# Feed-forward output of a four-layer decoder: seven block products per chunk in place of eight

## The chip, the cores and the metric

The kernel runs on one core of a Trainium2 chip. The metric is the device time of one execution in microseconds (us), of which several runs are taken. One execution was also recorded by the hardware profiler. The engines are TensorE (PE; PEld is its weight load), VectorE (DVE), ScalarE (ACT), GpSimd (POOL) and SyncE (SP), which issues the transfers (DMA).

## What is computed

Four decoder layers on 256 tokens of width 1024, in float32. Each layer has a feed-forward part, a token mixer (attention, gated linear attention, RWKV-7, attention) and another feed-forward part. The change is in the feed-forward parts alone, eight in all:

```python
def swiglu(x, w_in, w_out):
    gate, up = jnp.split(x @ w_in, 2, axis=-1)
    return (jax.nn.silu(gate) * up) @ w_out
...
        ff = swiglu(rmsnorm(h, g[0]), ffn_w_in[layer, 0], ffn_w_out[layer, 0])
        h = h + 0.5 * rmsnorm(ff, g[1])
```

`w_in` is 1024 x 5632, `w_out` is 2816 x 1024.

## The kernel before, in words

Each matmul of two float32 operands is made of three: an operand is split into a rounded part `hi` (a ScalarE copy) and a rest `lo` (a VectorE subtract), and `mm3` (L599) adds hi x hi, hi x lo and lo x hi. `weight` (L581) loads a 128 x 512 tile of weights and splits it so.

A feed-forward stage (`ffn`, L739) goes through the 2816 hidden values in 11 chunks of 256. The first two chunks (`OLD`) are done by `tokens` (L760) for each half of 128 tokens by itself, so that the first half can begin while the stage before still works on the second. There gate and up come out as 128 tokens x 512, go through VectorE, and are transposed on TensorE. The other nine chunks take both halves together: gate and up come out with the hidden values on the partitions, two PSUM banks per chunk, 96 matmuls of 256 columns. After the activation, `out` multiplies the hidden values with the chunk's 256 x 1024 piece of `w_out`. As blocks of 128 that is a 2 x 2 times 2 x 2 product: token half t, half i of the output columns, half j of the hidden values, 8 block products of three matmuls of 512 columns each. They add up in four PSUM banks, `acc[t][i]`, over all chunks; the other four banks rotate. At the end `postnorm` (L705) normalises each half's sum and adds it to the residual `h`.

No instruction stands where the program text has it. Every call is recorded with a due time, and a planner (`schedule`, L325) orders the calls of each engine by prices (`price`, L272) and by the free slots of each kind of tile: 87 `m` tiles of 512 columns, 14 `hf` of 256, 8 PSUM banks `ps`. Splits and loads may be put up to 24 us ahead of their due time. Where the planner sees TensorE idle behind a bank's release, it fills the time with matmuls of a tile of ones, which nothing reads (`o.fill`, L421, in fillers of 214 ns by its own price). All calls come out of `emit` (L458), so in the profile they share one line, L466, and the fillers have L464. An engine works its instructions off in the planned order: one that is late holds up what stands behind it.

## Time and profile before

| | us |
|---|---|
| median of 3 runs | 2063.19 (2063.02 to 2063.63) |
| the profiled execution | 2061.41 |
| its span, first to last instruction | 2059.4 |
| TensorE busy | 2041.0 (99%) |
| VectorE busy | 1415.6 (69%) |
| ScalarE busy | 1127.9 (55%) |
| GpSimd busy | 120.2 (6%) |
| DMA queue of SyncE | 352.78 MB, 55.1% of 16 engines' span |

A group of instructions is named by line, engine, operation and tiles (out<-in). Busy time is the union of the group's instructions; two that follow each other overlap, so that twelve of 0.69 us can take less than 12 x 0.69. A float32 matmul that is not split shows as two instructions, a filler too.

### The profile page before, as it was taken

The page shows a single profiled execution, that of the slowest core. Times are in us where ns is not written, and L with a number is a line of the kernel's source. Part 1 is how long each engine was busy: PE and PEld are TensorE (multiplying, and loading weights), DVE is VectorE, ACT ScalarE, POOL GpSimd, SP SyncE. Part 2 cuts the span into 40 slices and gives each one's busy share as a digit, 9 for nine tenths or more (in the row PEclk, how much of TensorE's full clock was granted, in tenths as well). Part 3 has the DMA queues.
Part 4 walks back from the last instruction along what each step waited for, and adds up shares of the span by engine and source line. Part 5 has one row for each costly group of instructions (what it writes and reads, how often), then busy time and mean ns, then how long its engine had stood idle before and what let it go on. Part 6 is the DMA issues. An engine that isn't in the chain of part 4 may idle for free.

```text
span 2059.4 us, 38914 instructions
## 1 busy us (share of the span) xinstructions
PE 2041.0 (99%) x14250; PEld 1792.2 (87%) x14250; DVE 1415.6 (69%) x2684; ACT 1127.9 (55%) x2408; POOL 120.2 (6%) x185
## 2 busy tenths in 40 slices
PE   9999999999999999999999999999999999999998
PEld 7998779998998888998899878888998899877997
DVE  7666886657666897666756797687666755688663
ACT  7444675446544965545554576566444544566442
POOL 0000000002000000000100022130000000000000
PEclk9999999999999999999999999999999999999999
DMA  9556365666555365566655521456566566536551
GB/s 299 179 184 200 125 191 173 189 186 196 176 184 186 117 186 184 175 188 201 190 179 179 155 87 63 126 168 189 180 185 209 168 186 204 163 122 204 174 185 66
DMA packets 288207, 355.25 MB, mean 173 GB/s; under 512 B 24156, under 2 KB 207632, under 8 KB 288016
## 3 DMA queue, kind: packets, MB, share of 16 engines
q1 hardware_dynamic: 288016, 352.78, 55.1%
q8 instruction: 111, 1.82, 0.4%
q14 instruction: 80, 0.66, 0.1%
HBM read 351.64 MB, written 1.05 MB: 171 GB/s over the span
## 4 chain that ended last, share of the span: by engine, by line
PE 86%; DVE 6%; ACT 2%; issue 2%; POOL 2%; DMA 1%; SPq 0%; DVEq 0%; POOLq 0%; ACTq 0%
PE ps L466 85%; DVE m L466 4%; POOL ti L466 2%; ACT m L466 1%; ACT junk L466 1%; DVE h L466 1%; DVE ti L466 1%; DMA h<-in_x_dram 0%; POOL m L466 0%; DMA m<-in_rwkv_a_dram 0%; PE ps L464 0%; DVE hf L466 0%; DMA m<-in_swa_w_o_dram 0%; SPq L466 0%; DMA m<-in_swa_w_qkv_dram 0%
## 5 line engine op out<-in xcount | busy, mean ns | idle before, releaser
L466 PE MATMUL ps<-m,m 128*128 128x256 f32 (+5 forms) x12128 | 1846.1, 316 | 3.9 <-ACT m L466 2.3
L466 PEld LDWEIGHTS ps<-m,m 128*128 128x128 f32 (+2 forms) x12128 | 1596.9, 185 | 192.6 <-issue 11.8
L466 ACT ACTIVATE m<-m 128x512 fp32r<-128x512 f32 (+3 forms) x1542 | 848.9, 617 | 608.7 <-DVE m L466 530.9
L466 DVE TENSOR_TENSOR m<-m,m 128x512 fp32r<-128x512 f32 (+2 forms) x1414 | 895.5, 687 | 101.6 <-ACT m L466 98.2
L466 DVE TENSOR_TENSOR m<-ps,m 128x512 f32<-128x512 f32 (+1 forms) x220 | 151.1, 690 | 377.4 <-PE ps L466 324.3
L466 ACT ACTIVATE m<-ps 128x512 f32<-128x512 f32 (+4 forms) x179 | 93.1, 547 | 133.4 <-PE ps L466 131.6
L466 POOL TENSOR_TENSOR ti<-ti,nhalf 128x1 f32<-128x1 f32 (+2 forms) x60 | 55.4, 924 | 1683.9 <-DVE ti L466 1516.1
L466 PE MATMUL ps<-m,hf 128*128 128x512 f32 (+1 forms) x716 | 124.5, 323 | 0.0
L466 PEld LDWEIGHTS ps<-m,hf 128*128 128x128 f32 (+1 forms) x716 | 83.1, 165 | 18.0 <-issue 3.1
L466 DVE SCALAR_TENSOR_TENSOR m<-m,m 128x512 f32<-128x512 f32 x102 | 69.7, 691 | 21.2 <-ACT m L466 14.9
L466 PE MATMUL ps<-ident,m 128*128 128x128 f32 (+1 forms) x344 | 57.5, 278 | 1.5 <-DVE m L466 0.6
L466 ACT ACTIVATE m<-ps,gT 128x128 fp32r<-128x128 f32 (+1 forms) x192 | 53.3, 378 | 3.6 <-PE ps L466 3.1
L466 ACT ACTIVATE hf<-ps,ti 128x256 f32<-128x256 f32 x32 | 15.1, 473 | 70.3 <-PE ps L466 70.2
L466 PEld LDWEIGHTS ps<-ident,m 128*128 128x128 f32 (+1 forms) x344 | 40.5, 142 | 14.9 <-DVE m L466 3.7
L466 POOL TENSOR_SCALAR_AFFINE_SELECT m<-m 128x512 f32<-128x512 f32 (+1 forms) x54 | 39.0, 742 | 190.4 <-ACT m L466 190.2
L466 DVE SCALAR_TENSOR_TENSOR m<-ps,gT,m 128x128 fp32r<-128x128 f32 x176 | 48.6, 343 | 1.9 <-ACT m L466 1.5
L466 ACT ACTIVATE junk<-h 128x512 bf16<-128x512 f32 x48 | 30.3, 631 | 22.1 <-DVE h L466 19.5
L466 ACT ACTIVATE junk<-ps 128x512 bf16<-128x512 f32 (+1 forms) x48 | 27.2, 567 | 27.3 <-PE ps L466 26.6
L466 DVE SCALAR_TENSOR_TENSOR h<-m,ti,h 128x512 f32<-128x512 f32 x48 | 34.2, 748 | 11.1 <-POOL ti L466 11.1
L466 DVE TENSOR_TENSOR m<-m,ps 128x256 f32<-128x256 f32 (+1 forms) x56 | 23.5, 455 | 26.1 <-PE ps L466 25.6
L466 ACT ACTIVATE hf<-ps 128x256 fp32r<-128x256 f32 (+4 forms) x54 | 19.8, 370 | 32.9 <-PE ps L466 32.9
L466 DVE SCALAR_TENSOR_TENSOR hf<-hf,ps 128x256 f32<-128x256 f32 x32 | 13.4, 418 | 33.9 <-ACT hf L466 33.8
(95 smaller groups left out, 574.3 us busy)
## 6 DMA issues: line engine op xcount, KB each, us to landing
m<-in_ffn_w_in_dram SPq DMA_DIRECT2D x704, 256.0 KB, 4.1
m<-in_ffn_w_out_dram SPq DMA_DIRECT2D x352, 256.0 KB, 5.1
m<-in_swa_w_qkv_dram SPq DMA_DIRECT2D x48, 256.0 KB, 3.6
m<-in_rwkv_w_rkv_dram SPq DMA_DIRECT2D x48, 256.0 KB, 3.2
m<-in_gla_w_in_dram SPq DMA_DIRECT2D x40, 256.0 KB, 3.5
m<-in_swa_w_o_dram SPq DMA_DIRECT2D x32, 256.0 KB, 2.8
m<-in_norm_g_dram SPq DMA_DIRECT2D x24, 256.0 KB, 5.2
m<-in_gla_w_o_dram SPq DMA_DIRECT2D x16, 256.0 KB, 2.7
```

Source lines behind the costliest of these rows:

```text
L466: getattr(getattr(self.nc, o.eng), fn)(*[fix(v) for v in args], **{k: fix(v) for k, v in kw.items()})
```

## The change

The four blocks of the hidden values and the four of `w_out` are combined so that seven block products per chunk are enough. `weights` makes four sums T of weight blocks on GpSimd (128 x 512 each) and splits three plain blocks and the four sums: seven splits per chunk where four were. `hidden` makes four sums S of hidden blocks on GpSimd (128 x 128 each) and splits three plain blocks and the four sums. `products` adds the seven products up in seven PSUM banks over all chunks. Gate and up of 128 hidden values share the eighth bank: it is filled, read and filled again in each chunk, and VectorE's and ScalarE's work on gate and up is done in two halves. The products follow one chunk behind. In the last four chunks (`TAIL`) the products 7 and 4, which only the second token half needs, are put off to the end. There seven VectorE sums and a copy make the four output blocks from the seven banks. The weights for a half chunk of gate and up are loaded in two transfers of 128 KB each (`load_half`), in place of one of 256 KB.

```diff
-MID = 8000.0
+MID = 16000.0
...
-LAST = 0
+LATE = 6000.0
+TAIL = 4
+
+AHEAD = 8000.0
+RESERVE = 16
...
         if fn == "tensor_tensor":
-            return 300 + 165.0 * n, 0.0
+            return 300 + 165.0 * n if args[3] == ALU.pow else 120 + 1.1 * n, 0.0
...
-                            if j >= len(f) or (t.first > front and occ[t.kind][front:t.first].max() + j >= bufs[t.kind]):
+                            keep = RESERVE if t.kind == "m2" and o.window is not None and o.key > now + AHEAD else 0
+                            if j + keep >= len(f) or (t.first > front and occ[t.kind][front:t.first].max() + j >= bufs[t.kind]):
...
-        nc.sync.dma_start(view(x) if view else x, src)
+        y = view(x) if view else x
+        for o, i in zip(y, src) if isinstance(src, list) else ((y, src),):
+            nc.sync.dma_start(o, i)
...
+        def load_half(c, j, k):
+
+            cols = slice(c * CH + j * P, c * CH + (j + 1) * P)
+            return self.weight([w_in[:, k + i, :, cols] for i in range(2)],
+                               lambda x: [x[:, i * CH:(i + 1) * CH].rearrange("p (s n) -> p s n", s=2) for i in range(2)])
...
+        def split(x, dt):
+
+            hi, lo = dt(), dt()
+            nc.scalar.activation(hi[:], x, AF.Copy)
+            nc.vector.tensor_tensor(lo[:], x, hi[:], ALU.subtract)
+            return hi, lo
+
+        def weights(c):
+
+            b = {}
+            nc.kind = "load"
+            for j in range(2):
+                for i in range(2):
+                    w = b[2 - j, i + 1] = self.m2()
+                    nc.sync.dma_start(w[:], w_out[:, 2 * c + j, i * 512:(i + 1) * 512])
+            nc.kind = "split"
+            T = {n: self.m2() for n in (1, 2, 3, 4)}
+            for n, x, y in ((1, b[1, 2], b[1, 1]), (2, b[2, 2], T[1]), (4, b[2, 1], T[2]), (3, b[2, 2], b[1, 2])):
+                GT(T[n][:], x[:], y[:], ALU.subtract)
+            r = {n: split(w[:], lambda: self.m2(dt=F32R)) for n, w in (
+                (1, b[1, 1]), (2, b[2, 1]), (3, b[2, 2]), (5, T[1]), (6, T[2]), (7, T[3]), (4, T[4]))}
+            nc.kind = None
+            return r
...
+        def hidden(th):
+
+            a12, a22, a11, a21 = (th[:, j, t, :] for j in range(2) for t in range(NT))
+            S = self.m2([P, 4, P])
+            s = [None] + [S[:, n, :] for n in range(4)]
+            GT(s[1], a21, a22, ALU.add)
+            GT(s[2], s[1], a11, ALU.subtract)
+            GT(s[3], a11, a21, ALU.subtract)
+            GT(s[4], a12, s[2], ALU.subtract)
+            three = th[:].rearrange("p j t n -> p (j t) n")[:, :3]
+            x = split(three, lambda: self.m2([P, 3, P], F32R))
+            y = split(S[:], lambda: self.m2([P, 4, P], F32R))
+            return {n: tuple(v[:, m, :] for v in z) for n, z, m in (
+                (1, x, 2), (2, x, 0), (4, x, 1), (5, y, 0), (6, y, 1), (7, y, 2), (3, y, 3))}
+
+        acc = {n: self.psum() for n in range(1, 8)}
+
+        def products(c, which):
+            w, x = wt[c], hid[c]
+            for n in which:
+                self.mm3(acc[n][:], x[n], tuple(v[:] for v in w[n]), c == 0, c == NCH - 1)
...
-            gh, gl = self.hf([P, CH], F32R), self.hf([P, CH], F32R)
-            nc.scalar.activation(gh[:], q[:, :CH], AF.Copy)
-            nc.vector.tensor_tensor(gl[:], q[:, :CH], gh[:], ALU.subtract)
-            for i in range(2):
-                for j in range(2):
-                    out(t, c, j, i, gh[:, j * P:(j + 1) * P], gl[:, j * P:(j + 1) * P])
-
-        rs, eps, acc, row = [None] * NT, [None] * NT, [None] * NT, self.m2()
+            nc.scalar.activation(ths[c][:, :, t, :], q[:, :CH].rearrange("p (j n) -> p j n", j=2), AF.Copy)
...
+        FIRST, SECOND = (1, 6, 5, 2), (3, 7, 4)
+        for c in range(OLD):
+            wt[c], hid[c] = weights(c), hidden(ths[c])
+            if c < OLD - 1:
+                products(c, FIRST + SECOND)
+        todo = list(range(OLD - 1, NCH))
+        for c in range(OLD, NCH):
+            for j in range(2):
+                p, half = self.psum(), {}
+                for s in range(2):
                     for k in range(KD):
...
+                        if k % 2 == 0 and s == 0:
+                            half[k // 2] = load_half(c, j, k)
+                        w, n = half[k // 2], (k % 2 * 2 + s) * P
+                        self.mm3(p[:, s * N:(s + 1) * N], (w.hi[:, n:n + P], w.lo[:, n:n + P]),
...
-            sg, th = self.m2([P, 2, N]), self.m2([P, 2, N])
-            two = lambda x: x[:].rearrange("p (j n) -> p j n", j=2)
-            nc.vector.tensor_tensor(sg[:], two(gate), row[:, :N].unsqueeze(1).to_broadcast([P, 2, N]), ALU.mult)
...
-            gh, gl = self.m2([P, 2, N], F32R), self.m2([P, 2, N], F32R)
-            nc.scalar.activation(gh[:], th[:], AF.Copy)
-            nc.vector.tensor_tensor(gl[:], th[:], gh[:], ALU.subtract)
...
+                sg, th, up = self.hf([P, N]), self.hf([P, N]), self.hf([P, N])
+                nc.vector.tensor_tensor(sg[:], p[:, :N], row[:, :N], ALU.mult)
+                nc.scalar.activation(up[:], p[:, N:], AF.Copy)
+                nc.scalar.activation(th[:], sg[:], AF.Tanh)
+                nc.vector.scalar_tensor_tensor(th[:], th[:], 1.0, sg[:], ALU.add, ALU.mult)
+                nc.vector.tensor_tensor(ths[c][:, j].rearrange("p t n -> p (t n)"), up[:], th[:], ALU.mult)
+                if j == 1:
+                    wt[c] = weights(c)
+                    hid[c] = hidden(ths[c])
+                products(todo[0], (FIRST, SECOND if todo[0] < NCH - TAIL else SECOND[:1])[j])
+            todo.pop(0)
         g = self.gain(n0 + 1, 16.0)
...
+        for n in FIRST + SECOND[:1]:
+            for c in todo:
+                products(c, (n,))
+        end = nc.base + nc.pe
+        s1, u2, u4 = self.m2(), self.m2(), self.m2()
+        c1, c2 = self.pair(), self.pair()
+        TT = nc.vector.tensor_tensor
+        nc.scalar.activation(s1[:], acc[1][:], AF.Copy)
+        TT(u2[:], s1[:], acc[6][:], ALU.add)
+        TT(u4[:], u2[:], acc[5][:], ALU.add)
+        TT(c1[0][:], s1[:], acc[2][:], ALU.add)
+        TT(c1[1][:], u4[:], acc[3][:], ALU.add)
+        self.postnorm(0, [x[:] for x in c1], g, eps[0][:, :1])
+        nc.base, nc.pe, nc.shift = end, 0.0, LATE
+        for n in SECOND[1:]:
+            for c in range(NCH - TAIL, NCH):
+                products(c, (n,))
+        TT(u2[:], u2[:], acc[7][:], ALU.add)
+        TT(c2[1][:], u4[:], acc[7][:], ALU.add)
+        TT(c2[0][:], u2[:], acc[4][:], ALU.add)
+        self.postnorm(1, [x[:] for x in c2], g, eps[1][:, :1])
         nc.shift = 0.0
```


How the planner's order moves, at three places. Names are the program's tiles with their numbers: `ps3` is the fourth PSUM bank, `m` an SBUF tile of 512 columns, `hf` one of 256.

First place, TensorE in the loop over chunks, where one half of gate and up is done and the bank is needed again. Before (`ps3_19` is gate, `ps6_21` up, `ps5_18` an output bank):

```order
L466 MATMUL ps3_19_642<-m226_27_205,m221_106_540 128x256
L466 MATMUL ps5_18_530<-m23_91_452,hf10_11_685 128x512
L466 MATMUL ps3_19_642<-m226_27_205,m211_103_507 128x256
L466 MATMUL ps3_19_642<-m230_31_223,m211_103_507 128x256
L466 MATMUL ps3_19_642<-m226_27_205,m222_107_544 128x256
L466 MATMUL ps6_21_737<-m219_20_180,m20_88_442 128x256
L466 MATMUL ps5_18_530<-m280_81_421,hf11_12_691 128x512
L466 MATMUL ps6_21_737<-m224_25_197,m20_88_442 128x256
L466 MATMUL ps6_21_737<-m219_20_180,m26_94_464 128x256
L466 MATMUL ps6_21_737<-m219_20_180,m21_90_449 128x256
L466 MATMUL ps6_21_737<-m224_25_197,m21_90_449 128x256
```

Now (`ps3_31` and `ps3_32` are two uses of the one bank; `ps5`, `ps1`, `ps4` are products 3, 7 and 4):

```order
L471 MATMUL ps3_31_1575<-m226_27_205,m232_311_1406 128x256
L471 MATMUL ps5_21_643<-m243_243_1071,m238_319_1456 128x512
L471 MATMUL ps5_21_643<-m211_275_1243,m238_319_1456 128x512
L471 MATMUL ps5_21_643<-m243_243_1071,m245_320_1464 128x512
L471 MATMUL ps1_22_657<-m268_252_1131,m238_319_1456 128x512
L471 MATMUL ps1_22_657<-m278_280_1263,m238_319_1456 128x512
L471 MATMUL ps1_22_657<-m268_252_1131,m245_320_1464 128x512
L471 MATMUL ps4_23_665<-m255_254_1140,m218_315_1434 128x512
L471 MATMUL ps4_23_665<-m263_281_1271,m218_315_1434 128x512
L471 MATMUL ps4_23_665<-m255_254_1140,m257_317_1445 128x512
L471 MATMUL ps3_32_1678<-m219_20_180,m274_308_1394 128x256
```

Two banks took turns, and single products stood between the matmuls of up; now nine products (twelve behind the other half) stand between two uses of one bank.

Second place, VectorE and GpSimd in the loop. VectorE before, from up of one chunk to gate of the next:

```order
L466 TENSOR_TENSOR m238_157_780<-ps6_21_737,m238_157_780 128x512
L466 TENSOR_TENSOR m275_170_837<-m234_163_807,m278_164_809 128x512
L466 TENSOR_TENSOR m256_172_848<-m238_157_780,m283_171_840 128x512
L466 TENSOR_TENSOR m271_175_857<-m272_166_816,m281_167_819 128x512
L466 TENSOR_TENSOR m255_178_866<-m267_168_823,m240_169_828 128x512
L466 TENSOR_TENSOR m253_181_875<-m268_173_853,m286_174_855 128x512
L466 TENSOR_TENSOR m23_182_879<-m282_176_861,m22_177_863 128x512
L466 TENSOR_TENSOR m280_183_884<-m277_179_869,m229_180_871 128x512
L466 TENSOR_TENSOR m20_186_910<-m25_184_906,m284_185_908 128x512
L466 TENSOR_TENSOR m29_189_922<-m26_187_918,m21_188_920 128x512
L466 TENSOR_TENSOR m27_192_934<-m24_190_930,m215_191_932 128x512
L466 TENSOR_TENSOR m210_193_939<-ps0_23_826,m213_102_504 128x512
```

VectorE now, from gate of one half chunk to gate of the next:

```order
L471 TENSOR_TENSOR hf0_29_1775<-ps3_32_1678,m25_93_457 128x256
L471 TENSOR_TENSOR m268_386_1779<-m247_348_1572,m20_360_1643 128x512
L471 SCALAR_TENSOR_TENSOR hf2_31_1784<-hf2_31_1784,hf0_29_1775 128x256
L471 TENSOR_TENSOR m218_387_1791<-hf1_30_1781,hf2_31_1784 128x256
L471 TENSOR_TENSOR m215_398_1815<-m250_353_1613,m280_362_1652 128x512
L471 TENSOR_TENSOR m239_401_1826<-m23_354_1617,m273_364_1673 128x512
L471 TENSOR_TENSOR m236_404_1847<-m270_355_1625,m216_365_1675 128x512
L471 TENSOR_TENSOR m248_409_1885<-m253_373_1715,m217_376_1724 128x512
L471 TENSOR_TENSOR m247_411_1890<-m251_374_1718,m234_377_1729 128x512
L471 TENSOR_TENSOR m235_413_1899<-m267_375_1721,m232_380_1743 128x512
L471 TENSOR_TENSOR m229_415_1904<-m286_378_1733,m243_382_1749 128x512
L471 TENSOR_TENSOR hf3_32_1907<-ps3_33_1824,m25_93_457 128x256
```

GpSimd now, one chunk; it had nothing there before:

```order
L471 TENSOR_TENSOR m215_340_1552<-m282_339_1550,m283_338_1548 128x512
L471 TENSOR_TENSOR m236_341_1554<-m233_337_1546,m282_339_1550 128x512
L471 TENSOR_TENSOR m239_342_1556<-m233_337_1546,m215_340_1552 128x512
L471 TENSOR_TENSOR m260_344_1560<-m242_336_1544,m239_342_1556 128x512
L471 TENSOR_TENSOR m252_368_1686<-m28_335_1542 128x128 x2
L471 TENSOR_TENSOR m252_368_1686<-m252_368_1686,m28_335_1542 128x128
L471 TENSOR_TENSOR m252_368_1686<-m28_335_1542,m252_368_1686 128x128
```

The read of a bank comes twice per chunk, with eight to nine splits queued between two of them; GpSimd has four sums of 512 columns in a row (T) and then four of 128 (S).

Third place, TensorE at the end of a stage. Before (`h0` is the residual of the first token half, whose transposes open the next stage):

```order
L466 MATMUL ps7_17_522<-m256_428_2144,m222_484_2446 128x512
L466 MATMUL ps5_18_530<-m270_431_2156,m258_483_2442 128x512
L466 MATMUL ps5_18_530<-m20_432_2158,m258_483_2442 128x512
L466 MATMUL ps5_18_530<-m270_431_2156,m222_484_2446 128x512
L466 MATMUL ps5_18_530<-m218_435_2171,m258_483_2442 128x512
L466 MATMUL ps5_18_530<-m247_436_2174,m258_483_2442 128x512
L466 MATMUL ps0_39_2514<-ident_77,h0_74 128x128 x4
L466 MATMUL ps4_40_2522<-ident_77,h0_74 128x128 x4
L466 MATMUL ps5_18_530<-m218_435_2171,m222_484_2446 128x512
L466 MATMUL ps3_41_2537<-m240_446_2248,m253_499_2528 128x512
```

Now (L469 is the fillers' line of the changed kernel):

```order
L471 MATMUL ps4_23_665<-m217_581_2735,m211_616_2887 128x512
L471 MATMUL ps4_23_665<-m23_595_2804,m211_616_2887 128x512
L471 MATMUL ps4_23_665<-m217_581_2735,m274_618_2896 128x512
L469 MATMUL ps3_42_2975<-ones_76 128x128 x13
L471 MATMUL ps3_42_2975<-ident_77,h0_74 128x128 x4
L471 MATMUL ps7_43_2996<-ident_77,h0_74 128x128 x4
L469 MATMUL ps0_44_3009<-ones_76 128x128
L471 MATMUL ps0_44_3009<-m255_583_2746,m269_640_3003 128x512
```

Products of the second token half stood before and behind the first half's transposes; now thirteen fillers stand there. In the whole program the fillers go from 48 to 115, beside 9 of the same kind at the start of both.

## Rows read from the trace of the kernel before

**Rows 1.** The page, parts 1 and 2: busy time, TensorE's granted clock in tenths.

```profile
PE 2041.0 (99%) x14250; PEld 1792.2 (87%) x14250; DVE 1415.6 (69%) x2684; ACT 1127.9 (55%) x2408; POOL 120.2 (6%) x185
...
PEclk9999999999999999999999999999999999999999
```

**Rows 2.** Waits of TensorE over the span: total us, times, longest.

```profile
PE ps L466 <- DVE hf L466: 2.6, 4, 0.7
PE ps L466 <- ACT m L466: 2.3, 1, 2.3
PE ps L466 <- DVE m L466: 2.0, 9, 0.3
```

**Rows 3.** Windows of one feed-forward stage: whole, its start, its loop.

```profile
core 0: us, PE busy (x) PEld busy (x) DVE busy (x) ACT busy (x) POOL busy (x), PEclk, DMA share, GB/s
471.00:662.00 191.00, 190.24 (x1255) 172.16 (x1255) 123.35 (x219) 96.88 (x196) 14.12 (x32) 1.00 0.58 182
471.00:509.00 38.00, 37.27 (x183) 30.06 (x183) 31.24 (x67) 25.00 (x62) 13.18 (x31) 1.00 0.59 184
542.00:640.00 98.00, 98.00 (x699) 91.85 (x698) 56.80 (x93) 43.71 (x80) 0.00 (x0) 1.00 0.57 179
```

**Rows 4.** Timeline of TensorE at 485 and 1160 us: start us, us, engine, instructions, count.

```profile
485.61 10.14 PE L466 MATMUL ps<-m,m 128*128 128x512 f32 x43
...
1160.46 2.39 PE L464 MATMUL ps<-ones 128*128 128x128 f32 x20
```

**Rows 5.** Groups by form, span: count, busy us, mean ns, idle before.

```profile
L466 PE MATMUL ps<-m,m 128*128 128x512 f32 x3696 | 940.8, 401 | 3.7 <-ACT m L466 2.3 <-DVE m L466 1.0
...
L466 DVE TENSOR_TENSOR m<-m,m 128x512 fp32r<-128x512 f32 x1340 | 855.0, 692 | 100.7 <-ACT m L466 97.5
...
L466 DVE TENSOR_TENSOR m<-ps,m 128x512 f32<-128x512 f32 x204 | 140.3, 690 | 370.8 <-PE ps L466 324.3 <-ACT m L466 34.9 <-ACT junk L466 11.0
...
L466 ACT ACTIVATE m<-m 128x512 f32<-128x512 f32 x128 | 78.5, 632 | 326.8 <-DVE m L466 326.5
...
L466 DVE TENSOR_TENSOR m<-m,ps 128x256 f32<-128x256 f32 x48 | 18.0, 417 | 25.1 <-PE ps L466 24.9
...
L464 PE MATMUL ps<-ones 128*128 128x128 f32 x96 | 12.7, 277 | 0.0
```

**Rows 6.** Timeline of ScalarE and VectorE at 307 us, of VectorE at 498 us.

```profile
306.98 6.35 ACT L466 ACTIVATE m<-m 128x512 fp32r<-128x512 f32 x12
...
307.64 7.32 DVE L466 TENSOR_TENSOR m<-m,m 128x512 fp32r<-128x512 f32 x12
...
498.32 8.51 DVE L466 TENSOR_TENSOR m<-m,m 128x512 fp32r<-128x512 f32 x12
```

**Rows 7.** Timeline of GpSimd and VectorE at 247, 498 and 1205 us.

```profile
247.50 0.63 POOL L466 TENSOR_SCALAR_AFFINE_SELECT m<-m 128x512 f32<-128x512 f32 x1 [38.54 <-ACT m L466]
...
498.40 3.56 POOL L466 TENSOR_SCALAR_AFFINE_SELECT m<-m 128x128 f32<-128x128 f32 x5
...
506.50 2.17 POOL L466 TENSOR_SCALAR_AFFINE_SELECT m<-m 128x128 f32<-128x128 f32 x3
...
1205.50 1.14 POOL L466 TENSOR_SCALAR_AFFINE_SELECT m<-m 128x512 f32<-128x512 f32 x1 [18.53 <-ACT m L466]
...
1206.05 1.13 DVE L466 TENSOR_TENSOR m<-m,m 128x512 fp32r<-128x512 f32 x1
...
1205.50 3.35 POOL L466 TENSOR_SCALAR_AFFINE_SELECT m<-m 128x512 f32<-128x512 f32 x4 [18.53 <-ACT m L466]
...
1207.11 1.27 DVE L466 TENSOR_TENSOR m<-ps,m 128x512 f32<-128x512 f32 x2
```

**Rows 8.** Page, part 3, and SyncE's issues at 463 us.

```profile
q1 hardware_dynamic: 288016, 352.78, 55.1%
...
463.22 1.98 SPq L466 DMA_DIRECT2D m<-in_ffn_w_out_dram  x4
466.09 6.48 SPq L466 DMA_DIRECT2D m<-in_ffn_w_in_dram  x8
```

More of the change, by code (lines that the diff above doesn't have):

```diff
@@ L746, in ffn @@
         uh, ul = ([self.m2([P, 2, NT, P], F32R) for _ in range(4)] for _ in "hl")
+        GT = nc.gpsimd.tensor_tensor
         def load_in(c, k):
@@ L750, in load_in @@
                 w_in[:, k, :, c * CH:(c + 1) * CH], lambda x: x.rearrange("p (s n) -> p s n", s=2)))
-        def load_out(c, j, i):
-            return self.once(("ffn", l, f, c, 8 + 2 * j + i), lambda: self.weight(
-                w_out[:, 2 * c + j, i * 512:(i + 1) * 512]))
-        def out(t, c, j, i, gh, gl):
-            w = load_out(c, j, i)
-            self.mm3(acc[t][i][:], (gh, gl), (w.hi, w.lo), c == 0 and j == 0, c == NCH - 1 and j == 1)
+        def load_half(c, j, k):
+            cols = slice(c * CH + j * P, c * CH + (j + 1) * P)
+            return self.weight([w_in[:, k + i, :, cols] for i in range(2)],
+                               lambda x: [x[:, i * CH:(i + 1) * CH].rearrange("p (s n) -> p s n", s=2) for i in range(2)])
@@ L773, in tokens @@
                 nc.tensor.transpose(q[:, j * P:(j + 1) * P], th[:, j * P:(j + 1) * P], self.ident[:])
-            gh, gl = self.hf([P, CH], F32R), self.hf([P, CH], F32R)
-            nc.scalar.activation(gh[:], q[:, :CH], AF.Copy)
-            nc.vector.tensor_tensor(gl[:], q[:, :CH], gh[:], ALU.subtract)
-            for i in range(2):
-                for j in range(2):
-                    out(t, c, j, i, gh[:, j * P:(j + 1) * P], gl[:, j * P:(j + 1) * P])
-        rs, eps, acc, row = [None] * NT, [None] * NT, [None] * NT, self.m2()
+            nc.scalar.activation(ths[c][:, :, t, :], q[:, :CH].rearrange("p (j n) -> p j n", j=2), AF.Copy)
+        rs, eps, row = [None] * NT, [None] * NT, self.m2()
+        ths = {c: self.m2([P, 2, NT, P]) for c in range(NCH)}
+        wt, hid = {}, {}
         nc.rate = 2
@@ L785, in ffn @@
             rs[t], eps[t] = self.ffn_prenorm(t, uh, ul, n0)
-            acc[t] = self.pacc(t)
             for c in range(OLD):
@@ L796, in ffn @@
         N = NT * P
-        last = NCH - (LAST if f == 0 else 0)
-        for c in range(OLD, last):
-            gate, up = self.psum(), self.psum()
-            for s, p in enumerate((gate, up)):
-                for j in range(2):
+        FIRST, SECOND = (1, 6, 5, 2), (3, 7, 4)
[8 more added lines that the diff above has]
+                for s in range(2):
@@ L813, in ffn @@
-            gh, gl = self.m2([P, 2, N], F32R), self.m2([P, 2, N], F32R)
-            nc.scalar.activation(gh[:], th[:], AF.Copy)
-            nc.vector.tensor_tensor(gl[:], th[:], gh[:], ALU.subtract)
-            for t in range(NT):
-                nc.shift = t * DEFER
-                for i in range(2):
-                    for j in range(2):
-                        out(t, c, j, i, gh[:, j, t * P:(t + 1) * P], gl[:, j, t * P:(t + 1) * P])
-                nc.shift = 0.0
-        g = self.gain(n0 + 1, 16.0)
@@ L823, in ffn @@
-        start, end = nc.base + nc.pe, 0.0
-        if last < NCH:
-            nc.rate = 2
-        for t in range(NT):
-            nc.base, nc.pe, nc.shift = start, 0.0, t * DEFER
-            for c in range(last, NCH):
-                tokens(t, c)
-            end = end or nc.base + nc.rate * nc.pe
-            self.postnorm(t, [x[:] for x in acc[t]], g, eps[t][:, :1])
+                sg, th, up = self.hf([P, N]), self.hf([P, N]), self.hf([P, N])
+                nc.vector.tensor_tensor(sg[:], p[:, :N], row[:, :N], ALU.mult)
```

6 lines of the change are left out of this document (removed).

## The prediction

> **What bounds the kernel now.** I read the page first, then the engines' busy time in a stretch of the program, then the groups of instructions, then the timeline of single stretches.
>
> On the page, TensorE is busy 2041.0 of 2059.4 us, at a granted clock that stands at 9 or more tenths in every slice [rows 1]. The waits of TensorE for other engines are short: the three largest sums are 2.6, 2.3 and 2.0 us [rows 2]. So nothing ends late: TensorE is the bound, nearly everywhere, and a matmul that goes away is time gained, as long as every other engine can follow. VectorE is at 69% and GpSimd at 6%. That second engine is the one to watch, because the change gives it work.
>
> The windows show one whole feed-forward stage (471 to 662 us): 191 us, TensorE busy 190.24, VectorE 123.35, ScalarE 96.88 [rows 3]. Eight such stages make up most of the span. The stretch 542 to 640 lies inside the loop over chunks: 699 matmuls in 98.00 us, all of it busy. A chunk there has 96 matmuls of 256 columns and 24 of 512, 120 in all, so it takes 98.00 x 120 / 699 = 16.8 us. 43 matmuls of 512 columns in a row take 10.14 us [rows 4]; the last one shows its 0.40 us latency [rows 5], so one follows the other after (10.14 - 0.40) / 42 = 0.232 us.
>
> **The change, part by part.**
>
> *TensorE.* Per chunk 7 x 3 matmuls of 512 columns take the place of 8 x 3. Over 11 chunks and 8 stages that is 264 fewer, which is also what the two orders give; 264 x 0.232 = 61.2 us less, or 7.7 per stage. The gate and up matmuls keep their number and size. Against that, the planner now sets 115 filler matmuls behind the warm-up where it had 48, most of them at the ends of the stages, where the products that used to cover the way from the accumulators to the next stage's transposes are gone. Twenty filler instructions, two to a filler, take 2.39 us [rows 4], 0.28 of it the last one's own [rows 5], so a filler takes 2 x (2.39 - 0.28) / 19 = 0.222 us: 67 x 0.222 = 14.9 us more, 1.9 per stage. By TensorE alone a stage would go from 191 to 185.2 us, and the execution from 2061.4 to 2015 us.
>
> *The last bank.* Gate and up share one bank that is used twice per chunk. Between its last matmul and the next use stand 9 or 12 products: 2.1 or 2.8 us. In that time VectorE must read the gate (0.42 us for 256 columns [rows 5]) and ScalarE the up half. That fits with about 1 us to spare if VectorE comes at once. It is hidden by the products, but if VectorE is more than that behind, TensorE stands at the bank, where it had two banks in rotation before.
>
> *ScalarE* gets 592 instructions more. At no more than 0.63 us each [rows 5] that is 47 us per stage, 144 of 185: no bound. I cost it at nothing.
>
> *VectorE.* The orders differ by: 312 more subtracts of SBUF tiles of 512 columns, at 7.32 / 12 = 0.61 us when they follow each other [rows 6]: +190. 432 more instructions of 256 columns, at 0.42 [rows 5]: +181. 88 of 384 columns, between those two, taken as 0.52: +46. 192 fewer of 512 columns, with a PSUM input or of the three-operand form, at 0.69 and 32 fewer of 256: -146. Sum +271 us, 34 per stage, so VectorE's work per stage goes from 123.35 to 157.3 us. That still fits into 185.2.
>
> *GpSimd, the cost that decides.* Per chunk it now subtracts or adds four tiles of 512 columns and four of 128, 2560 columns; 28160 per stage. None of it is on TensorE's path by itself. But GpSimd and VectorE do not run beside each other. In rows 7, a select of 512 columns that takes 0.63 us alone takes 1.14 us while VectorE works on two SBUF tiles, and VectorE's subtract of 512 columns, begun in that time, takes 1.13 instead of 0.69 [rows 5]: 0.44 us lost for 512 columns, 0.86 ns per column. The two took turns. Twelve subtracts beside 14 selects of 128 columns (the first five and the last three stand in rows 7) took 8.51 us, against 7.32 without [rows 6]: 1.19 us for 14 x 128 columns, 0.66 ns per column. Two VectorE instructions that read PSUM, beside the same chain of selects, took 1.27 us, undisturbed. So every column that GpSimd handles is taken from VectorE when VectorE has two SBUF inputs, which is about 87% of its new time (48 instructions of a stage, some 21 of 157.3 us, read PSUM).
>
> What a subtract of two tiles costs on GpSimd no row shows; its only two-input rows are powers of one to eight columns, another operation. Below, it is as quick per column as the select, 0.66 to 0.86 ns. Above, its two operands are read one behind the other, twice that, 1.72. I take the upper end: the select is the nearest row in size, and its time goes with the columns that it reads; the subtract reads two. VectorE's time with the turns is then
>
> - low end: 157.3 + 0.87 x 28160 x 0.86 ns = 178.4 us per stage, less than TensorE's 185.2;
> - high end: 157.3 + 0.87 x 28160 x 1.72 ns = 199.4 us, more than the 191 of today.
>
> VectorE and TensorE meet at 185.2 us at 1.14 ns per column. VectorE can also not be busy all of a stage: at its start (471 to 509) it stood idle 6.8 of 38 us, waiting for small chains [rows 3]. I keep half, 3.4 us, and get 202.8, 11.8 us above today. Eight stages: **+94 us**, the 61 us saved on TensorE being idle time there. 2061.4 + 94.4 = 2155.8; the median lies 1.8 us above the profiled execution, **2158**.
>
> The Trainium skill (GPSIMD Engine Reference, section 3.1) has a price: 4497 ns for an fp32 add of two tiles of 2048 columns, 2.2 ns per column, and lays it to one read port that takes the operands in turn. No run here shows it. By that price, called an estimate, a stage would need 211 us on VectorE before any idle time, and the sum would come to some 2250 us; by the rows' upper end it is 2158. Page and rows point the same way, against this change.
>
> *Loads.* The weights of gate and up now come in 16 transfers per chunk of 128 KB with 512-byte runs, where there were 8 of 256 KB. SyncE issues 8 in 6.48 us at most, 4 of the output weights in 1.98 [rows 8]: 16 x 0.81 + 4 x 0.50 = 15 us per chunk of 16.1. It fits, so I cost it at nothing; behind a waiting issue, though, all other loads stand. The bytes are the same.
>
> **The rivals.**
>
> *GpSimd is quick enough (faster).* If it needs less than 1.14 ns per column, VectorE fits into TensorE's 185.2 us, and the saved matmuls count: 2015 us, plus what the shared bank costs at a VectorE that is 96% busy. 144 uses late by 0.1 to 0.2 us make 15 to 30: about **2035**, between 2015 and 2055. For it: the planner's own price for these operations is 120 + 1.1 ns per column, 0.68 us for 512, and its other prices agree with the rows (ScalarE 0.52 against 0.53, VectorE 0.60 against 0.61 [rows 6], the select 0.61 against 0.63 [rows 7]). Against it: two operands. Chance 0.30.
>
> *The two cancel (no change).* At about 1.37 ns per column VectorE takes the 191 us of today: **2063**, within 4 us. Chance 0.08; it is a narrow band.
>
> *Loads bind (slower, another way).* If a transfer's time goes by its pieces and not by bytes: 288016 packets at 55.1% of 16 engines' span [rows 8] are 63 ns each; 2048 more per chunk are 8.1 us on top of 0.57 x 16.8, 17.7 us in a chunk of 16.1, so 72 x (17.7 - 16.8): **2124**. The share of 0.57 to 0.59 today [rows 3] leaves room, and half the bytes should take less time. Chance 0.05.
>
> **How the numbers follow.** The forecast, VectorE and GpSimd taking turns as the bound, has 0.57. Its own range: at 1.52 ns (twice the mean of 0.66 and 0.86) and no idle time 194.5 per stage, 2091; at 1.72 with all VectorE work in turns and all the idle time, 205.7 + 6.8 per stage, 2233. Over all cases I give 2020 to 2235: the quick GpSimd lies at the low end, and what is left out is a still dearer subtract above and a gain without any new wait below. Faster by over 0.2% (about what a measurement of this kernel can tell from no change): 0.30. Within it: 0.08. Slower: 0.57 + 0.05 = 0.62.
>
> **What would show it.** GpSimd's subtract of 128x512: above 1.1 us means the forecast, 0.7 to 0.8 the first rival. VectorE's 128x512 subtract: a mean well above 0.69 us. VectorE's share: from 69% to over 85%, TensorE's down to some 92%. TensorE's waits: long ones at the last bank, released by VectorE's read or ScalarE's copy of it, by the hundred. A chunk (117 matmuls) at 17 to 18 us, against 16.1 by TensorE. The matmul spacing must stay 0.232. If VectorE's subtracts keep 0.69 us while GpSimd works, my reading of rows 7 is wrong, and with it the forecast; if the waits are released by DMAs, it is the loads.

## The result, and the profile after

| | before | after |
|---|---|---|
| median of 4 runs, us | 2063.22 (2063.02 to 2063.63) | 2398.24 (2397.45 to 2399.71) |
| span of the profiled execution, us | 2059.4 | 2395.5 |
| mean granted clock | 0.999 | 0.958 |

The changed kernel takes 1.162 times as long (interval 1.160 to 1.164). The page, parts 1 and 2, where [rows 1] stood:

```profile
PE 2109.6 (88%) x14120; PEld 1818.6 (76%) x14120; DVE 2029.5 (85%) x3292; ACT 1368.8 (57%) x3000; POOL 899.8 (38%) x889
...
PEclk8999999999999999999999999999999999999998
```

TensorE has fallen from 99% to 88%, and VectorE has risen from 69% to 85%. Neither is full. The waits over the span, for [rows 2], with those of GpSimd, ScalarE and VectorE (us in total, times, longest):

```profile
ACT m L471 <- POOL m L471: 335.2, 197, 5.5
ACT hf L471 <- DVE hf L471: 284.4, 121, 8.3
...
DVE m L471 <- ACT m L471: 158.1, 120, 2.7
...
PE ps L471 <- ACT hf L471: 139.1, 83, 4.2
PE ps L471 <- DVE hf L471: 91.1, 33, 6.2
...
DVE hf L471 <- ACT hf L471: 85.0, 132, 6.7
```

TensorE's two largest waits are 230 us together. The groups by form tell where they stand:

```profile
L471 PE MATMUL ps<-m,m 128*128 128x256 f32 x6984 | 922.5, 294 | 185.5 <-ACT hf L471 139.1 <-DVE hf L471 45.7 <-DVE m L471 0.3
...
L471 PE MATMUL ps<-ident,hf 128*128 128x128 f32 x66 | 15.0, 310 | 45.4 <-DVE hf L471 45.4
```

Ahead of the gate and up matmuls, which need the shared bank, TensorE stands 185 us (139.1 + 45.7). The other 45 us stand ahead of transposes that wait for VectorE. The waits close a circle: TensorE waits for ScalarE and VectorE, VectorE for ScalarE, ScalarE for GpSimd and VectorE. The windows of the stage that answers to [rows 3], its start and the whole:

```profile
core 0: us, PE busy (x) PEld busy (x) DVE busy (x) ACT busy (x) POOL busy (x), PEclk, DMA share, GB/s
554.00:592.00 38.00, 32.22 (x135) 23.43 (x135) 33.67 (x61) 23.14 (x59) 22.38 (x19) 0.96 0.42 125
554.00:788.00 234.00, 201.59 (x1264) 175.97 (x1264) 200.90 (x304) 131.83 (x285) 108.56 (x121) 0.96 0.51 152
```

The stage takes 234 us and not 191. VectorE works 200.9 us of it, 1.5 us more than the forecast of 199.4; but it stands idle 33.1 us, where the forecast left 3.4. The tile view of hf and of m shows who loses time (count; min/median/max in ns):

```profile
L471 DVE TENSOR_TENSOR hf<-ps,m x144: 406/414/425, 61.7 to 2376.1; 128x256 f32<-128x256 f32 x144
L471 DVE SCALAR_TENSOR_TENSOR hf<-hf,hf x144: 411/426/1530, 63.4 to 2377.2; 128x256 f32<-128x256 f32 x144
```

```profile
L471 POOL TENSOR_TENSOR m<-m,m x528: 449/1448/3827, 24.1 to 2379.9; 128x512 f32<-128x512 f32 x97, 128x128 f32<-128x128 f32 x79
```

Same engine, same number of columns: the instruction that reads PSUM never takes over 425 ns, the one with two SBUF inputs up to 1530. One chunk in the timeline:

```profile
102.02 5.95 POOL L471 TENSOR_TENSOR m<-m,m 128x512 f32<-128x512 f32 x4 [5.12 <-DMA m<-in_ffn_w_out_dram]
102.10 7.62 PEld L471 LDWEIGHTS ps<-m,m 128*128 128x128 f32 x57 [1.16 <-ACT hf L471]
...
102.39 1.28 DVE L471 SCALAR_TENSOR_TENSOR hf<-hf,hf 128x256 f32<-128x256 f32 x1 [0.16 <-ACT hf L471]
103.70 1.40 DVE L471 TENSOR_TENSOR m<-hf,hf 128x256 f32<-128x256 f32 x1
105.03 6.50 DVE L471 TENSOR_TENSOR m<-m,m 128x512 fp32r<-128x512 f32 x7
...
111.46 0.41 DVE L471 TENSOR_TENSOR hf<-ps,m 128x256 f32<-128x256 f32 x1
111.90 0.38 ACT L471 ACTIVATE hf<-ps 128x256 f32<-128x256 f32 x1 [2.22 <-DVE hf L471]
...
112.34 8.72 PE L471 MATMUL ps<-m,m 128*128 128x256 f32 x60 [2.18 <-ACT hf L471]
...
116.62 2.72 ACT L471 ACTIVATE m<-m 128x512 fp32r<-128x512 f32 x5 [2.49 <-POOL m L471]
117.28 3.70 DVE L471 TENSOR_TENSOR m<-m,m 128x512 fp32r<-128x512 f32 x6 [1.56 <-ACT m L471]
...
121.79 1.45 PE L471 MATMUL ps<-m,m 128*128 128x256 f32 x10 [0.73 <-ACT hf L471]
121.80 1.30 POOL L471 TENSOR_TENSOR m<-m,m 128x512 f32<-128x512 f32 x1 [5.21 <-DMA m<-in_ffn_w_out_dram]
```

From 102.10 to 121.79 a chunk takes 19.7 us, against 16.8 before. Four GpSimd sums of 512 columns start at 102.02. Beside them VectorE takes 1.28 + 1.40 + 6.50 = 9.18 us for what takes 0.43 + 0.43 + 7 x 0.61 = 5.13 alone: 4.05 us lost, 1.01 per sum. Only then, at 111.46, comes its read of the gate half; ScalarE copies the up half behind it, and TensorE stands 2.18 us. At 117.28 VectorE itself stands 1.56 us, behind ScalarE, which waits for the sums of hidden blocks. So in one chunk VectorE is too late in one place and idle in another.

The loads do not bind: TensorE waits 0.7 us for a transfer in the whole span, ScalarE 11.7 for the feed-forward weights. GpSimd waits 194.6 us for output weights ahead of its sums; in `sums_one_input` below it waits 247.4 us for them, and that kernel is 279 us faster. The page, parts 3 and 6, for [rows 8]:

```profile
q1 hardware_dynamic: 444688, 352.82, 48.9%
...
m<-in_ffn_w_in_dram SPq DMA_DIRECT2D x1152, 128.0 KB, 2.9
```

### The profile page after: what moved, and what is told of

Its sections match the earlier page's. It is cut to its first block, busy times and chain, and to the rows that moved or that the text cites. A ratio compares the mean times of both kernels' runs of the same rounds, so it can differ in the third digit from the quotient of the medians.

```text
span 2395.5 us, 41720 instructions
## 1 busy us (share of the span) xinstructions
PE 2109.6 (88%) x14120; PEld 1818.6 (76%) x14120; DVE 2029.5 (85%) x3292; ACT 1368.8 (57%) x3000; POOL 899.8 (38%) x889
## 2 busy tenths in 40 slices
DMA packets 444902, 355.47 MB, mean 148 GB/s; under 512 B 33372, under 2 KB 364304, under 8 KB 444688
## 3 DMA queue, kind: packets, MB, share of 16 engines
q1 hardware_dynamic: 444688, 352.82, 48.9%
## 5 line engine op out<-in xcount | busy, mean ns | idle before, releaser
L471 PE MATMUL ps<-m,m 128*128 128x256 f32 (+4 forms) x12248 | 1976.2, 326 | 217.4 <-ACT hf L471 139.1
L471 PEld LDWEIGHTS ps<-m,m 128*128 128x128 f32 (+2 forms) x12248 | 1665.7, 193 | 457.8 <-ACT hf L471 177.6
L471 DVE TENSOR_TENSOR m<-m,m 128x512 fp32r<-128x512 f32 (+1 forms) x1814 | 1385.1, 816 | 148.3 <-ACT m L471 144.8
L471 ACT ACTIVATE m<-m 128x512 fp32r<-128x512 f32 (+4 forms) x1838 | 1003.8, 610 | 437.0 <-POOL m L471 335.2
L471 POOL TENSOR_TENSOR m<-m,m 128x512 f32<-128x512 f32 (+1 forms) x528 | 656.9, 1258 | 351.3 <-DMA m<-in_ffn_w_out_dram 194.6
L471 POOL TENSOR_TENSOR m<-m 128x128 f32<-128x128 f32 x176 | 131.1, 764 | 534.2 <-DVE m L471 321.1
L471 ACT ACTIVATE hf<-ps 128x256 f32<-128x256 f32 (+1 forms) x166 | 62.3, 377 | 266.4 <-DVE hf L471 244.4
L471 DVE SCALAR_TENSOR_TENSOR hf<-hf,hf 128x256 f32<-128x256 f32 x144 | 99.6, 692 | 60.1 <-ACT hf L471 60.0
L471 DVE TENSOR_TENSOR m<-hf,hf 128x256 f32<-128x256 f32 x144 | 115.5, 802 | 5.0
L471 DVE TENSOR_TENSOR m<-m,ps 128x512 f32<-128x512 f32 (+1 forms) x112 | 60.4, 568 | 25.3 <-PE ps L471 23.3
L471 PEld LDWEIGHTS ps<-ident,hf 128*128 128x128 f32 x68 | 7.9, 148 | 55.1 <-DVE hf L471 38.9
```

The costliest lines, as they stand in the source:

```text
L471: getattr(getattr(self.nc, o.eng), fn)(*[fix(v) for v in args], **{k: fix(v) for k, v in kw.items()})
```

## The experiments

Times are of one execution each; the kernel before took 2062.45 to 2063.76 us beside them. Three theories at first. A: the turns with VectorE cost the time, once VectorE is full. B: the waits for GpSimd's results do. C: it is the shared bank, the splits and the stages' ends. T are the four sums of weight blocks (128x512) of a chunk, S the four of hidden blocks (128x128).

| run | us | VectorE busy, us | granted clock |
|---|---|---|---|
| before | 2062.69 | 1415.6 | 0.999 |
| after | 2398.24 | 2029.5 | 0.958 |
| no_sums | 2041.49 | 1664.2 | 0.994 |
| sums_unread | 2351.96 | 2064.2 | 0.956 |
| sums_one_input | 2119.59 | 1772.6 | 0.985 |
| sums_on_vectore | 2119.71 | 1937.9 | 0.985 |
| before_half_dose | 2224.77 | 1777.8 | 0.979 |
| t_subtracts_out | 2286.85 | 1801.3 | 0.967 |
| turns_in_the_plan | 2370.27 | 2063.5 | 0.956 |

**The sums taken out, made idle, made simpler, moved.** `no_sums` leaves T and S out, and the splits read loaded and hidden blocks:

```diff
-                GT(T[n][:], x[:], y[:], ALU.subtract)
...
-            GT(s[1], a21, a22, ALU.add)
...
-                (... (5, T[1]), (6, T[2]), (7, T[3]), (4, T[4]))}
+                (... (5, b[1, 2]), (6, b[2, 2]), (7, b[2, 2]), (4, b[2, 1]))}
```

> The eight sums of blocks per chunk (T and S) are left out; the seven splits and seven products take plain blocks in their place. Theory A (VectorE and GpSimd take turns, so GpSimd's sums are taken from VectorE): all the loss goes, 2015 to 2045 us, granted clock back to 0.99 or more. Theory B (the engines stand in planned order behind a late GpSimd result, the turns matter little): the same, 2015 to 2045. Theory C (the shared bank, the added splits and the ends of the stages cost it, GpSimd only runs beside): still above 2200.

`sums_unread` keeps T and S and has the same inputs of the splits as no_sums, so nothing reads them.

> GpSimd makes all its sums as in the change, but nothing reads them: splits and products take plain blocks. Theory A: VectorE loses the same time to GpSimd, 2250 to 2400 us, VectorE's 512-column subtracts still with a mean near 0.81 us. Theory B: nobody waits for a sum any more, so 2015 to 2080. Between the two, the share of each can be read off.

`sums_one_input` puts a select of one operand in the place of each sum:

```diff
-                GT(T[n][:], x[:], y[:], ALU.subtract)
+                SEL(T[n][:], y[:], 512)
```

> Each GpSimd sum is replaced by a select of one tile of the same size (a copy), so the order of the chain T1, T2, T4 and s1, s2, s4 stays, while each takes about 0.63 us alone instead of 1.27 (128x512). By the prediction's threshold of 1.14 ns per column VectorE then fits (178 us per stage), and the time is 2020 to 2060. If waits in planned order behind GpSimd matter as much as the sum of VectorE's time, it stays above 2100.

`sums_on_vectore`:

```diff
-        GT = nc.gpsimd.tensor_tensor
+        GT = nc.vector.tensor_tensor
```

> The same kernel with the sums T and S on VectorE; the output is the same. VectorE per stage: 157 + 11 x (4 x 0.61 + 4 x 0.2) = 193 us, a little above the 191 of the kernel before, and no turns. Theory A: 2070 to 2130 us. Theory B: the chain T to split gets shorter too, 2040 to 2080. Theory C: above 2300, as the bank and the splits are as in the change.

Measured 2041.49, 2351.96, 2119.59 and 2119.71 us. Without its sums the change is 21 us faster than the kernel before, so C falls: bank, splits and ends cost 26 us over the 2015 of TensorE's path, no more. Of the 357 us that the sums cost, 310 are there when nothing reads them, and 46 come with the reading. That speaks for A over B, but the 310 need not be turns alone. GpSimd is also one more reader of loaded tiles: SyncE, which loads them anew, waits 188.6 us for it in sums_unread, 34.3 in after, and ScalarE waits 68.0 us for gate and up weights there, 3.0 in after. And the selects should have ended at 2020 to 2060, and cost 78 us with VectorE at 84%. That speaks against "once VectorE is full". The pages, part 1, of no_sums and sums_unread, and that wait of SyncE in sums_unread:

```profile
PE 2001.1 (98%) x14114; PEld 1761.2 (86%) x14114; DVE 1664.2 (82%) x3292; ACT 1354.2 (66%) x3000; POOL 117.3 (6%) x185
```

```profile
PE 2101.7 (89%) x14098; PEld 1816.1 (77%) x14098; DVE 2064.2 (88%) x3292; ACT 1362.5 (58%) x3000; POOL 943.9 (40%) x889
```

```profile
SPq L471 <- POOL m L471: 188.6, 52, 12.7
```

The turns take 400 us from VectorE in 8 x 28160 columns, 1.78 ns each, while its instructions are the same 3292. On VectorE itself the sums are 274 us of work and cost only 78.

**Nearly the same GpSimd work in the kernel before** (theory W: in-order engines hand a delay on although none is full). before_half_dose has 352 sums of 128x512, as the change (8 of them take a tile from itself and stand in a group of their own), and 288 of 128x128, where the change has 352; its edit:

```diff
+                nc.gpsimd.tensor_tensor(dead[:], raws[-1][:], raws[0][:], ALU.subtract)
...
+            for s in range(4):
+                nc.gpsimd.tensor_tensor(dead[:, s * P:(s + 1) * P], th[...], th[...], ALU.subtract)
```

> The kernel before, with eight GpSimd sums per chunk added whose results nothing reads (four of 128x512 on the output weights, four of 128x128 on the hidden blocks): the same GpSimd work as the change, nothing else. Theory A (VectorE loses about 2.1 ns per GpSimd column, and only a full VectorE costs time): VectorE's 123 us of a stage become about 175, still under TensorE's 191, so 2060 to 2085 us. Theory W (a late VectorE costs TensorE at once, through the banks that it must read, long before it is full): two banks in rotation soften it, but 2100 to 2200 us. A granted clock below 0.98 would speak for W.

> The kernel before with idle GpSimd sums again, this time in the change's number: per chunk four of 128x512 and four of 128x128 (the run before_idle_sums turned out to hold nearly eight of 128x512, 688 in all, not four). Theory A (GpSimd costs time only where it makes VectorE full): VectorE's 965 us in the feed-forward stages become about 1310 of 1520, so 2063 to 2095 us. Theory W (in-order engines: each delay of VectorE reaches TensorE although VectorE is not full): in proportion to the double dose, 2062 + 0.52 x 429 = 2285, at least 2150 us.

Measured 2490.99 (double dose, 688 sums of 128x512) and 2224.77. This decides against "once it is full". The page, part 1, waits of ScalarE and TensorE, of SyncE, and groups by form, of before_half_dose:

```profile
PE 2098.7 (94%) x14250; PEld 1809.7 (81%) x14250; DVE 1777.8 (80%) x2684; ACT 1156.9 (52%) x2408; POOL 875.5 (39%) x825
```

```profile
ACT m L466 <- DMA m<-in_ffn_w_in_dram: 180.5, 153, 3.6
...
PE ps L466 <- ACT m L466: 42.3, 24, 3.4
PE ps L466 <- DVE m L466: 37.6, 56, 2.8
```

```profile
SPq L466 <- POOL m L466: 278.8, 88, 8.5
```

```profile
L466 POOL TENSOR_TENSOR m<-m,m 128x512 f32<-128x512 f32 x344 | 548.7, 1595 | 30.8 <-DMA m<-in_ffn_w_out_dram 4.9
...
L466 DVE TENSOR_TENSOR m<-m,m 128x512 fp32r<-128x512 f32 x1340 | 1191.8, 942 | 81.0 <-ACT m L466 76.0
```

The old kernel, whose VectorE had a third of its time free, loses 161 us to idle GpSimd sums with VectorE at 80%. Its two-input subtract went from 692 ns [rows 5] to 942. Not all of the 161 is the turns' doing: ScalarE waits 180 us for gate and up weights, 10 before, and SyncE, which loads them, now waits 278.8 us for GpSimd to be done with a buffer. How the 161 us divide between the two is not shown.

**What the bank does.** `two_banks` and `bank_freed_by_scalare`:

```diff
+        acc[7] = acc[4]
```

```diff
-                nc.vector.tensor_tensor(sg[:], p[:, :N], row[:, :N], ALU.mult)
-                nc.scalar.activation(up[:], p[:, N:], AF.Copy)
+                nc.scalar.activation(gu[:], p[:], AF.Copy)
+                nc.vector.tensor_tensor(sg[:], gu[:, :N], row[:, :N], ALU.mult)
```

> The changed kernel with products 4 and 7 added into one accumulator (so the two are not kept apart, and the output is not the reference's): the same matmuls, sums and splits, but two banks in rotation for gate and up. Theory A (VectorE is the bound): VectorE's work is the same, so 2350 to 2400 us. Theory W (the one bank, with VectorE's read and ScalarE's copy behind it, turns VectorE's lateness into waits of TensorE): TensorE's 139 us of waits for ScalarE's copy and most of the 91 us for VectorE's results shrink: 2150 to 2300 us.

> The changed kernel with gate and up copied out of the shared bank by one ScalarE instruction, and VectorE's gate product reading the copy in SBUF: TensorE's wait at the bank no longer stands behind VectorE's queue. If that queue is where the lateness reaches TensorE and there alone: 230 us of waits for hf shrink by more than half, 2230 to 2320 us. If the lateness only moves on (to the low parts that the products read, as in two_banks): 2370 to 2430 us.

Measured 2392.63 and 2412.13. Neither gains anything. TensorE's groups by form, first two_banks, then bank_freed_by_scalare:

```profile
L471 PE MATMUL ps<-m,m 128*128 128x512 f32 x3816 | 1084.1, 426 | 127.5 <-ACT m L471 101.6 <-DVE m L471 24.9
L471 PE MATMUL ps<-m,m 128*128 128x256 f32 x6984 | 895.6, 288 | 60.6 <-DVE m L471 60.4
```

```profile
L471 PE MATMUL ps<-m,m 128*128 128x512 f32 x3816 | 1039.0, 414 | 64.0 <-ACT m L471 44.2 <-DVE m L471 18.9
L471 PE MATMUL ps<-m,m 128*128 128x256 f32 x6984 | 913.0, 291 | 152.1 <-ACT m L471 140.1 <-DVE m L471 11.7
```

With a second bank the waits for hf ahead of gate and up are gone, and TensorE stands ahead of matmuls of 512 columns, the products' size, instead (127.5 us, where it was 31.5). In the other run it still stands at the bank: 140.1 us for ScalarE's copy, which has ScalarE's queue in front of it (298 us of waits for GpSimd). So it is two_banks that speaks against the bank as the cause.

**What the clock does.** In after, TensorE's mean granted clock is 0.958: at two levels, 1.2 and 2.4 GHz, it had the lower one for 2 x (1 - 0.958) x 2395.5 = 201 us, which at half speed loses at most 100 us of work. In the one fall followed here, TensorE had waited 4.53 us for VectorE, up to 607.33 us, and from 608 to 610 us it was granted 0.50. `clock_kept` gives it something to do in the waits at the bank:

```diff
+                    for _ in range(5):
+                        nc.tensor.matmul(spare[:, :P], lhsT=self.ones[:], rhs=self.ones[:], start=True, stop=True)
```

> The changed kernel with five filler matmuls ahead of each use of the shared bank in the loop, written to a bank of their own (made free by adding products 4 and 7 into one accumulator, so the output is not the reference's): TensorE has work in the waits at the bank. Theory C (the falls to the lower clock, 193 us of them in these stages with TensorE busy 84% of that, cost up to 81 us): granted clock above 0.98 and 2310 to 2360 us. Theory L (VectorE is the pace, TensorE's clock matters little): 2380 to 2420 us, whatever the clock.

Measured 2421.93 at a granted clock of 0.975: the time at the lower clock fell to 2 x 0.025 x 2420.2 = 121 us, and the kernel became no faster. But the fillers have a cost of their own:

```profile
L471 PE MATMUL ps<-m,m 128*128 128x256 f32 x6984 | 886.4, 286 | 96.2 <-ACT hf L471 93.3 <-DVE m L471 2.8
L471 PE MATMUL ps<-ones 128*128 128x128 f32 x1458 | 187.3, 277 | 1.1 <-POOL ones L471 1.1
```

They add some 152 us of TensorE's time (187.3 against 30.9 + 4.2 in after), and the waits at the bank fall by only 89 us (185.5 to 96.2). So this run does not show what the lower clock costs by itself; the bound is 100 of the 335 us that the change costs. GpSimd's sums cost time without it, too: `block_sums_on_vectore` below, at a granted clock of 0.990 (44 us at the lower level), is 87 us slower than sums_on_vectore at 0.985 (64 us).

**Which sums, and VectorE's load.** `block_sums_on_vectore` (T on VectorE), `hidden_sums_on_vectore` (S) and `t_subtracts_out`:

```diff
-                GT(T[n][:], x[:], y[:], ALU.subtract)
+                nc.vector.tensor_tensor(T[n][:], x[:], y[:], ALU.subtract)
```

```diff
+            GT = nc.vector.tensor_tensor
             GT(s[1], a21, a22, ALU.add)
```

```diff
+                nc.scalar.activation(hi[:], w[:], AF.Copy)
+                r[n] = hi, r[o][1]
```

> The four sums of weight blocks of 128x512 per chunk on VectorE, the four of hidden blocks of 128x128 on GpSimd. With all sums on GpSimd 2398 us, with all on VectorE 2120. Theory A: GpSimd keeps a fifth of its columns, so a fifth of the loss by turns, while VectorE is spared some 0.8 us of work per chunk: 2110 to 2160 us. Theory of waits for GpSimd's results (its chain of four hidden sums, before the splits): 2200 to 2300 us.

> The reverse of block_sums_on_vectore: the four sums of hidden blocks on VectorE, the four of weight blocks on GpSimd. Theory H (the chain of hidden sums on GpSimd keeps ScalarE and then VectorE waiting, about 2 us per chunk in the timeline): 2230 to 2320 us, the 87 us that lie between 2207 and 2120 come off 2398. Theory A alone (turns, no waits): VectorE gains some 0.8 us of sums per chunk and loses as much by turns, so 2375 to 2410 us.

> The changed kernel without VectorE's four subtracts per chunk that make the low parts of the block sums (the low part of a plain block stands in, so the output is not the reference's); GpSimd's sums and ScalarE's copies stay. Theory L (VectorE's own stream, its work and the waits in it, is the pace; TensorE's waits at the bank follow from it): 352 x 0.82 = 288 us of VectorE's time go, so 2090 to 2190 us. If the pace is set by GpSimd's sums and the chains behind them: above 2280 us.

Measured 2207.13, 2336.33 and 2286.85. Against all sums on VectorE (2119.71), S on GpSimd costs 87 us, T on GpSimd 217, both 279: the parts nearly add up, and a fifth of the columns make nearly a third of the cost. S stands inside the chain that ScalarE and VectorE wait for: with S alone on GpSimd, ScalarE waits for it 226.8 us. Without the low parts VectorE has 228 us less to do (2029.5 - 1801.3) and the kernel is only 111 us faster, VectorE at 79%: theory L (VectorE's own stream, its work and the waits in it, is the pace) falls too: its range ended at 2190.

**What the order does.** `dear_sums_planned`, `turns_in_the_plan` (and the same with S on VectorE), and T in two places:

```diff
-            return 300 + 165.0 * n if args[3] == ALU.pow else 120 + 1.1 * n, 0.0
+            return 300 + 165.0 * n if args[3] == ALU.pow else 120 + 2.3 * n, 0.0
```

```diff
+            if o.turn:
+                d += max(0.0, lock - s)
+                lock = s + d - 100.0
```

```diff
-                if j == 1:
+                if j == 0:
                     wt[c] = weights(c)
+                else:
+                    weights2(c)
```

> The changed kernel with other prices for the planner alone: GpSimd's sum of 512 columns 1.30 us in place of 0.68, VectorE's two-tile sum of 512 columns 0.86 in place of 0.60. Theory P (the order is written for quick sums, and the in-order engines wait in the wrong places): 2200 to 2330 us, with a granted clock above 0.97, since fillers now stand where TensorE waits. Theory A or W: the work is the same, 2360 to 2420 us.

> The changed kernel, the same work, with a planner that knows the turns: a GpSimd sum and a VectorE instruction with two SBUF inputs are planned one after the other, a sum of 512 columns at 1.30 us. Theory W (the turns cost so much because they come where the written order does not expect them, with TensorE's next read queued behind): 2180 to 2320 us. Theory Q (GpSimd's sums in the loop cost as much wherever they stand, since a chunk's chains through four in-order engines leave no room): 2370 to 2430 us.

> As turns_in_the_plan, and the four sums of hidden blocks on VectorE. Without the planner's knowledge this split gave 2336. Theory W: 2130 to 2270 us. Theory Q: 2310 to 2350 us.

> The changed kernel with its four sums of weight blocks issued in two pairs, one in each half of the chunk, in place of four in a row: same work. Theory B (four turns in a row, some 4.3 us of VectorE's time at once, push its gate read past the bank's cover of 2.1 to 2.8 us, and two would not): 2250 to 2330 us. If the sum of the turns counts, wherever they stand: 2370 to 2430 us.

> Both: sums of weight blocks in two pairs, and the planner that knows the turns (2370 by itself). Theory B: 2210 to 2310 us. If the sum of the turns counts: 2350 to 2400 us.

Measured 2426.83, 2370.27, 2321.60, 2436.85 and 2466.24. Dearer prices for single operations make it worse, and so do two pairs of T sums. A planner that knows that the two engines take turns, with GpSimd's sums at the dearer price, gains 28 us, 15 with S on VectorE, of the 279 that GpSimd costs over VectorE. So most of it is not a wrong order that this planner could mend.

**The best version that makes all sums.** `sums_on_vectore_bank_by_scalare` is both edits together.

> All sums on VectorE (2120 us by itself) and the bank freed by one ScalarE copy, the version with most of the new waits taken out that still makes every sum. TensorE waits little at the bank there (some 20 us), so 2095 to 2125 us; below 2063 would make the change worth keeping, and I do not expect it.

Measured 2118.26, 2.7% over the kernel before. Even with no sums at all only 21 us are to be had, and none of the versions tried here that make every sum beats the old kernel.

## Why the prediction was wrong

- **Direction, and the cause: right.** Slower, through GpSimd and VectorE taking turns: VectorE is busy 365 us longer than without the sums, with the same instructions, and 310 of the 357 us that the sums cost are there with results that nobody reads (buffers held by GpSimd have an unknown part in that run). VectorE's PSUM reads stay undisturbed (425 ns at most), as [rows 7] had it. The Trainium skill (SBUF — State Buffer, "SBUF: two separate sides") calls it an exclusive lock, held for a whole instruction, that VectorE needs for two SBUF inputs; the 425 and 1530 ns of the tile view agree.
- **TensorE's path: right.** 37 matmuls of 512 columns take 8.85 us in no_sums: (8.85 - 0.40) / 36 = 0.235 us, forecast 0.232. That kernel ends at 2041 where the path alone gave 2015.
- **VectorE's own new work: right.** Forecast +271 us, no_sums shows 1664.2 - 1415.6 = 249.
- **Price of a GpSimd column: nearly right on the whole, too low for one sum.** I took 1.72 x 0.87 = 1.50 ns per column; VectorE lost (2029.5 - 1664.2) us / 225280 (8 x 28160 columns) = 1.62. A single sum costs more: 1.30 us for 512 columns in the timeline (at 121.80 us), 0.449 for 128 [tile view above], 2.2 ns per column; a part of them falls on idle time or PSUM reads of VectorE. The price is not the main miss, since VectorE's work per stage came out right. The Trainium skill (GPSIMD Engine Reference, section 3.1) has 4497 ns for 2048 columns, 2.2 ns per column, and these rows agree. By its price the sum came to some 2250 us, an estimate, and 2398 is beyond that too.
- **The step that failed: "I keep half, 3.4 us, and get 202.8".** I let a stage last as long as VectorE works, plus the little idle time of the stage's start. VectorE's work was right to 1.5 us a stage, partly by luck: its own new work was 2.8 us less than forecast and the turns took 3.5 more. The idle time is 33.1. 8 x (33.1 - 3.4) = 238 us, and the median missed the forecast by 240.
- **The threshold failed with it: "VectorE and TensorE meet at 185.2 us at 1.14 ns per column".** By the forecast, 1.14 ns on GpSimd take 0.87 x 1.14 = 0.99 ns per column from VectorE. The selects take (1772.6 - 1664.2) us / 225280 = 0.48, half of that, and cost 78 us; before_half_dose costs 161 with VectorE at 80%. No engine has to be full. The explanation, argued and not shown by a run: TensorE has next to no slack of its own, so what a turn delays on its path is lost, and VectorE's free time lies elsewhere in a fixed order.
- **The last bank: "about 1 us to spare if VectorE comes at once".** VectorE does not come at once, and 185 us of TensorE's waits stand there. Yet a second bank saved no time: the bank is where the delay shows and not its cause.
- **ScalarE at nothing: not quite.** 57% busy, it bounds nothing; but its copies stand in order behind GpSimd's sums (335 us of waits), which is part of how VectorE comes to be idle.
- **Rivals.** GpSimd quick enough and the cancelling fall with 1.30 us per sum. Loads bind: 128 KB land in 2.9 us (256 KB took 4.1), and 54% more packets (444688) raised the queue's time by 3%: 48.9% of 2395.5 us is 1171, 55.1% of 2059.4 was 1135. A packet's time does not stay at 63 ns.
- **Not in the sum: the clock.** 201 us at the lower level, at most 100 us of work, and the fall followed above came behind a wait. Fillers that kept the clock up more cost at least what they gained.

What stays open: which link of the chunk's chains sets 19.7 us in all stages. In the last stage's loop the profile has a chain from 2215 us on, and one chunk of it lasts 19.66 us; by line, for 2241.14 to 2260.80:

```profile
by line: DVE m L471 53.2%; POOL m L471 15.0%; DMA m<-in_ffn_w_in_dram 13.0%; DVE hf L471 5.8%; issue 4.8%; ACT hf L471 4.4%; ACT m L471 3.7%; ACTq L471 0.1%
```

It goes round through VectorE (59%), GpSimd's sums S (15%) and ScalarE (8%), and TensorE is not in it. The load in it is not shown to bind, since VectorE was working through the same 2.6 us, on two instructions that the sums T had lengthened. So there a ring of in-order engines, none of them full, sets the pace. For the other stages it is what remains, by elimination: a second bank, dearer prices and sums in pairs gained nothing, and for the clock there is only the bound.
